# Moving weights stored as even and odd halves, and read from the two halves by turns

## The chip, the cores and the metric

The kernel runs on one core of one Trainium2 chip (trn2). The metric is the device time in microseconds of one execution; smaller is better. Three runs of the kernel before took 576.83, 577.91 and 578.27 us, a median of 577.91 us.

## The reference

A two-layer decoder trunk over 256 tokens with 1024 features, all in float32. Layer 0 is block-sparse attention with 16 heads (with 256 tokens there is one block, so it is plain causal attention). Layer 1 is sliding-window attention with window 128, four shared key/value heads and learned sinks. Each layer ends with a gated feed-forward block whose hidden rows pass a causal convolution of width 3:

```
for l in range(DEPTH):
    h = rmsnorm(x, attn_norm[l])
    if l < N_A:                       # layer 0
        q, k, v = split(h @ w_qkv_a[l], 3);  o = moba_attention(rope(q), rope(k), v)
    else:                             # layer 1
        k, v = split(rmsnorm(x, kv_norm) @ w_kv_b, 2)
        o = swa_sink_attention(rope(h @ w_q_b), rope(k), v, sinks_b)
    x = x + o @ w_o
    u = causal_conv3(rmsnorm(x, ffn_norm[l]) @ w_up[l])      # 1024 -> 2 x 2816
    gate, val = split(u, 2)
    x = x + (silu(gate) * val) @ w_down[l]                   # 2816 -> 1024
return rmsnorm(x, final_norm)
```

## The kernel before

**Products in three.** [...] To keep float32 accuracy, each operand is split into a high part (ScalarE copies it to float32r, L157) and a low part (VectorE subtracts, L160), and each product is three matmuls: high by high, high by low, low by high. In the profile `wh`/`wl` are the parts of a weight unit, and the tiles called `q` hold the parts of activations.

**Weight units.** The host packs all weights into 92 units of 128 partitions x 2048 columns (`pack`), 1 MB each. SyncE's queue fetches a unit into one of three `raw` buffers; ScalarE and VectorE make `wh` and `wl` in pieces; four pairs of them are in use or ready. When TensorE has used a unit, `used(i)` lets the preparation of unit i+4 begin. Tiles from `spaced` start 4 elements (16 bytes) into a buffer that is 64 elements longer than its content.

**Two kinds of matmul.** In the first kind the weights are stationary and the activations are the moving operand, 256 columns (the tokens): the q and k projections of layer 0 (`proj_f`, L445 to L447) and the up projections (L715 to L717). In the second kind the activations are stationary, 128 tokens at a time, and the weights are the moving operand. The second kind is what the change touches:

| place | lines | what | moving columns | matmuls |
|---|---|---|---|---|
| `v_first` | L827 | first half of layer 0's v, while weights still come in | 512 | 48 |
| `proj` | L317 to L319 | second half of v; layer 1's k and v | 512 | 96 |
| `proj` | L317 to L319 | layer 1's q, four groups | 256 | 192 |
| `Down.mm` | L621, L622, L626 | both attention outputs and both down projections | 512 | 714 |
| `Down.end` | L681 to L683 | last quarter of the last down projection | 256 | 12 |

Each matmul reads its columns one after the other from consecutive addresses of SBUF and adds to a PSUM bank in the same order.

**Order.** The order on each engine is fixed when the program is built. A small planner counts TensorE time (`tick`) and puts the conversions and the post-processing at due times between the matmuls. During attention, the softmax of one head pair runs beside matmuls that a `filler` generator gives: the other q/k groups, v, and the first units of the output projection.

Of the kernel before, what the change touches and what calls it, by code (L numbers as in the profile page):

```python
# [14 lines left out]
P = 128  # L15
D = 1024
S = 256
NB = S // P
KC = D // P
NH = 16  # L20
HD = 64
# [39 lines left out]
def trunk(ctx: ExitStack, tc, x, xw, pos, cpk, fin, sinks, w, out):  # L61
    nc = tc.nc
# [28 lines left out]
    def bank(tag):  # L91
        return ps.tile([P, 512], F32, tag=tag, name=nm(tag), bufs=4 if tag == "acc" else 2)
# [4 lines left out]
    def blk(b):  # L97
        return slice(b * P, (b + 1) * P)

    def half(n):  # L100
        return slice(n * 512, (n + 1) * 512)

# [11 lines left out]
    def tick(ns):  # L116
        clock[0] += ns
        while put_off and not busy[0]:
            item = min(put_off, key=lambda t: t[0])
            if item[0] > clock[0]:  # L120
                return
            run_item(item)
# [13 lines left out]
    def require(*key):  # L136

        while True:
            mine = [t for t in put_off if t[1] == key]
            if not mine:  # L140
                return
            run_item(min(mine, key=lambda t: t[0]))
# [45 lines left out]
    def used(i):  # L188

        prepare(i + 4)  # L190

    def need(i):
        require("w", i)
# [5 lines left out]
    first = [wp.tile([P, UNIT], F32, tag="raw", name=f"first{i}", bufs=3) for i in range(3)]  # L199
# [42 lines left out]
    for b in range(NB):  # L242
        t = one.tile([P, NH, HD], F32, name=f"v{b}")
# [62 lines left out]
    def hx(hT, c):  # L306
        hi, lo = hT[c // 4]
        return hi[:, c % 4], lo[:, c % 4]

    def proj(o, hT, b, wv, units=()):  # L310

        n = o.shape[-1]
        for c in range(KC):
            require("x", b, c // 4)
            xh, xl = hx(hT, c)
            wh, wl = wv(c)
            nc.tensor.matmul(o, xh[:, blk(b)], wh, start=(c == 0), stop=False)  # L317
            nc.tensor.matmul(o, xh[:, blk(b)], wl, start=False, stop=False)
            nc.tensor.matmul(o, xl[:, blk(b)], wh, start=False, stop=(c == KC - 1))  # L319
            tick(3 * n / 2.4)  # L320
            if units and (c + 1) * len(units) % KC == 0:
                used(units[(c + 1) * len(units) // KC - 1])
            yield 3 * n / 2.4
# [278 lines left out]
    class Down:  # L602
# [6 lines left out]
        def mm(self, i, k, b, cols):  # L609
            if self.acc is None:  # L610
                self.acc = [[bank("acc") for _ in range(2)] for _ in range(NB)]
            need(self.u + i)
            self.wait(i)
            hi, lo = wq[self.u + i]
            ph, pl = self.parts[2 * i + k]
            first = i == 0 and k == 0
            end = k == 1 and (i == self.n_u - 1 or i == self.n_u - 2 and self.short and (b, cols[0][0]) == (1, 1))
            for n, c in cols:
                o = self.acc[b][n][:, c]
                s_ = slice(k * D + n * 512 + c.start, k * D + n * 512 + c.stop)  # L620
                nc.tensor.matmul(o, ph[:, blk(b)], hi[:, s_], start=first, stop=False)  # L621
                nc.tensor.matmul(o, ph[:, blk(b)], lo[:, s_], start=False, stop=False)  # L622
            for n, c in cols:
                o = self.acc[b][n][:, c]
                s_ = slice(k * D + n * 512 + c.start, k * D + n * 512 + c.stop)
                nc.tensor.matmul(o, pl[:, blk(b)], hi[:, s_], start=False, stop=end)  # L626
            tick(len(cols) * 3 * (c.stop - c.start) / 2.4)

        def units(self, lo, hi):
# [37 lines left out]
        def end(self, b, n, tail):  # L667

            i = self.n_u - 1
            require("x", b, n)  # L670
            x_ = xr[b][:, half(n)]
            nc.vector.tensor_tensor(out=x_, in0=self.acc[b][n], in1=x_, op=ALU.add)
            need(self.u + i)
            self.wait(i)
            wh, wl = wq[self.u + i]
            for m in range(2):
                o = bank("u")[:, :S]
                for k in range(2):
                    ph, pl = (t[:, blk(b)] for t in self.parts[2 * i + k])
                    c = slice(k * D + n * 512 + m * S, k * D + n * 512 + (m + 1) * S)  # L680
                    nc.tensor.matmul(o, ph, wh[:, c], start=(k == 0), stop=False)  # L681
                    nc.tensor.matmul(o, ph, wl[:, c], start=False, stop=False)
                    nc.tensor.matmul(o, pl, wh[:, c], start=False, stop=(k == 1))  # L683
                tick(640)
                tail(m, o)

# [9 lines left out]
    def ffn(layer, u_up, u_dn, hT, y, rb, after, tail=None):  # L696
# [72 lines left out]
        for cs_ in (range(4), range(4, KC)):  # L769
            for i in range(2):  # L770
                mm(i, ups[i], cs_)
# [5 lines left out]
        for i in range(2, NF):  # L777
            if i % 2 == 0:
                pq = quad()
            up = bank("acc" if i < 4 else "t" if i % 2 else "u")  # L780
            mm(i, [up[:, :S], up[:, S:]], range(KC))
            used(u_up + i)
            post(i, [up[:, :S], up[:, S:]], pq)
# [35 lines left out]
    v_acc = [bank("acc") for _ in range(NB)]  # L819

    def v_first(c):
        xh, xl = hx(hT, c)
        s_ = slice((c % 4) * 512, (c % 4 + 1) * 512)
        wh, wl = (t[:, s_] for t in wq[c // 4])
        for k, (a, m) in enumerate(((xh, wh), (xl, wh), (xh, wl))):
            for b in range(NB):
                nc.tensor.matmul(v_acc[b], a[:, blk(b)], m, start=(c == 0 and k == 0), stop=(c == KC - 1 and k == 2))  # L827
        tick(1280)

    def v_out(b, n, o):  # L830
# [124 lines left out]
    def v_half(n, u):  # L955
        for b in range(NB):
            o = bank("acc")
            yield from proj(o, hT, b, cols512(u), (u, u + 1) if b else ())
            chain(("v", n), (150.0, lambda b=b, o=o: v_out(b, n, o)))
# [71 lines left out]
    for b in range(NB):  # L1031
        o = bank("acc")
# [94 lines left out]
def pack(inp):  # L1127

    import numpy as np

    def k_major(m):
        return m.reshape(m.shape[0] // P, P, m.shape[1])

    units = []
    m = k_major(inp["w_qkv_a"][0])
    q, k, v = (m[:, :, i * D:(i + 1) * D] for i in range(3))
    qk = [np.concatenate([q[:, :, g * 256:(g + 1) * 256], k[:, :, g * 256:(g + 1) * 256]], axis=2) for g in range(4)]
    blocks = [v[:, :, :512], qk[0], qk[1], qk[2], v[:, :, 512:], qk[3]]

    def halves(blk):  # L1140
        for a in range(2):
            units.append(blk[4 * a:4 * a + 4].transpose(1, 0, 2).reshape(P, UNIT))

    def rows2(mat):
        mm = k_major(mat)
        for i in range(mm.shape[0] // 2):
            units.append(mm[2 * i:2 * i + 2].transpose(1, 0, 2).reshape(P, UNIT))

    def up(mat):
        mm = k_major(mat).reshape(KC, P, 2, NF, P)  # L1150
        for i in range(NF):
            units.append(mm[:, :, :, i].transpose(1, 0, 2, 3).reshape(P, UNIT))

    for blk in blocks:
        halves(blk)
    rows2(inp["w_o_a"][0])
    up(inp["w_up"][0])
    rows2(inp["w_down"][0])
    halves(k_major(inp["w_kv_b"]))

    order = [(2 * (j // 4) + e) * 4 + j % 4 for j in range(NH // 2) for e in range(2)]
    m = k_major(inp["w_q_b"][0].reshape(D, NH, HD)[:, order].reshape(D, D))
    for g in range(4):
        units.append(m[:, :, g * 256:(g + 1) * 256].transpose(1, 0, 2).reshape(P, UNIT))
    rows2(inp["w_o_b"][0].reshape(NH, HD, D)[order].reshape(D, D))
    up(inp["w_up"][1])
    rows2(inp["w_down"][1])
    assert len(units) == N_UNITS
    wpk = np.stack(units)

    def feat(v_):
        return v_.reshape(-1, P).T

    cols = [feat(v_) for v_ in (inp["kv_norm"], inp["attn_norm"][1],
                                inp["ffn_norm"][0], inp["ffn_norm"][1])]
    for l in range(2):
        four = np.concatenate([inp["conv_w"][l], inp["conv_b"][l][None]], axis=0)
        cols.append(four.reshape(4, 2 * NF, P).transpose(2, 1, 0).reshape(P, 2 * NF * 4))
    cpk = np.concatenate(cols, axis=1)
    return {  # L1180
        "x": inp["x"].reshape(S, D),
        "xw": np.concatenate([feat(inp["attn_norm"][0])] + [
            t for c in range(KC) for t in (inp["x"].reshape(S, KC, P)[:, c].T, blocks[0][c])], axis=1),
        "pos": inp["positions"].reshape(NB, P).T,
        "cpk": cpk,
        "fin": inp["final_norm"],
        "sinks": inp["sinks_b"].reshape(NH)[order],
        "w": wpk,
    }
# [19 lines left out]
```

## Time and profile before

| what | value |
|---|---|
| time, median of 3 runs | 577.91 us (576.83 to 578.27) |
| span of the profiled execution, first to last instruction | 576.2 us; the median run stands 1.7 us above it (the profiled execution's own device time is not listed) |
| PE (matmul) busy | 560.7 us, 4022 instructions |
| VectorE / ScalarE / GpSimd busy | 438.0 / 379.5 / 103.5 us |
| HBM read | 99.30 MB, 174 GB/s over the span |
| mean granted TensorE clock | 0.989 |

PE counts as busy while any matmul is in flight, and neighbouring matmuls overlap: a row that says that one matmul took 390 ns does not mean that the next starts 390 ns later. How fast TensorE really goes is read from the distance between the starts of neighbouring matmuls, in the timeline and in the chain of waits. The chain of waits leads back from the last instruction of the program to what held each step.

### The profile page before, as it was taken

Reading aid. Unit: us, or ns where it says so; the run is one execution under the profiler, and the core shown is the slowest. Engines: PE = TensorE matmul, PEld = TensorE weight load, DVE = VectorE, ACT = ScalarE, POOL = GpSimd, SP = SyncE. Lnnn points to the kernel's source line nnn. Section 1 sums busy time; section 2 is a strip of 40 time slices with the busy share of each in tenths; the row PEclk is TensorE's granted clock in tenths of the full one; section 3 lists DMA queues with packets and bytes.
Section 4 is the critical chain, followed back from the end, with each engine's and each line's share of the span. In section 5 each row is a group of like instructions: output and inputs, shape, how many; then the busy total and the mean of one; then the engine's idle time right before and its main releaser. Section 6 shows DMA issues by size and latency. Waiting matters only on the chain.

```text
span 576.2 us, 10530 instructions
## 1 busy us (share of the span) xinstructions
PE 560.7 (97%) x4022; PEld 514.7 (89%) x4022; DVE 438.0 (76%) x928; ACT 379.5 (66%) x771; POOL 103.5 (18%) x130
## 2 busy tenths in 40 slices
PE   9789999999999999999999999999999999999995
PEld 7679889789999999988887988779999999988884
DVE  6579988678899888864449989778988888873414
ACT  6845987777567776752439788887666777663313
POOL 8221102002233223110000100001322322110003
PEclk9889999999999999999999999999999999999998
DMA  8834462532384656664551732323365556665201
GB/s 326 345 110 183 148 239 82 197 140 93 128 289 159 220 211 220 220 208 175 202 207 46 270 136 94 127 97 124 110 222 212 204 214 216 251 215 204 95 0 73
DMA packets 15312, 101.00 MB, mean 175 GB/s; under 512 B 1952, under 2 KB 2080, under 8 KB 3744
## 3 DMA queue, kind: packets, MB, share of 16 engines
q1 hardware_dynamic: 14976, 100.09, 48.5%
q8 instruction: 31, 0.51, 0.3%
q10 hardware_dynamic: 288, 0.26, 0.1%
q14 instruction: 17, 0.14, 0.1%
HBM read 99.30 MB, written 1.05 MB: 174 GB/s over the span
## 4 chain that ended last, share of the span: by engine, by line
PE 89%; ACT 3%; DVE 3%; DMA 2%; issue 1%; POOL 1%; SPq 0%; DVEq 0%; POOLq 0%; ACTq 0%
PE acc L621 9%; PE acc L622 9%; PE acc L626 9%; PE u L715 6%; PE u L717 6%; PE u L716 6%; PE t L717 6%; PE t L715 6%; PE t L716 6%; PE acc L447 2%; PE acc L445 2%; PE acc L446 2%; PE acc L715 2%; PE acc L717 2%; PE acc L716 2%; PE acc L317 2%
## 5 line engine op out<-in xcount | busy, mean ns | idle before, releaser
L160 DVE TENSOR_TENSOR wl<-wr,wh 128x1024 fp32r<-128x1024 f32 (+1 forms) x208 | 223.1, 1090 | 69.9 <-ACT wh L157 68.7
L157 ACT ACTIVATE wh<-wr 128x1024 fp32r<-128x1024 f32 (+1 forms) x208 | 189.6, 945 | 68.7 <-PE acc L626 56.5
L759 POOL TENSOR_TENSOR m<-m,m 128x256 f32<-128x256 f32 x44 | 63.8, 1449 | 177.2 <-DVE m L754 111.6
L621 PE MATMUL acc<-wh,q 128*128 128x512 f32 x238 | 94.3, 396 | 0.0
L622 PE MATMUL acc<-wl,q 128*128 128x512 f32 x238 | 92.8, 390 | 0.0
L715 PE MATMUL u<-q,wh 128*128 128x256 f32 x320 | 88.4, 277 | 0.0
L716 PE MATMUL u<-q,wh 128*128 128x256 f32 x320 | 88.2, 276 | 0.0
L717 PE MATMUL u<-q,wl 128*128 128x256 f32 x320 | 88.0, 275 | 0.0
L717 PE MATMUL t<-q,wl 128*128 128x256 f32 x288 | 79.2, 275 | 0.0
L715 PE MATMUL t<-q,wh 128*128 128x256 f32 x288 | 79.2, 275 | 0.0
L716 PE MATMUL t<-q,wh 128*128 128x256 f32 x288 | 79.2, 275 | 0.0
L626 PE MATMUL acc<-wh,q 128*128 128x512 f32 x238 | 77.1, 389 | 0.0
L716 PEld LDWEIGHTS u<-q,wh 128*128 128x128 f32 x320 | 60.1, 188 | 0.0
L717 PEld LDWEIGHTS u<-q,wl 128*128 128x128 f32 x320 | 60.1, 188 | 0.0
L715 PEld LDWEIGHTS u<-q,wh 128*128 128x128 f32 x320 | 59.9, 188 | 0.0
L717 PEld LDWEIGHTS t<-q,wl 128*128 128x128 f32 x288 | 54.1, 188 | 0.0
L715 PEld LDWEIGHTS t<-q,wh 128*128 128x128 f32 x288 | 54.1, 188 | 0.0
L716 PEld LDWEIGHTS t<-q,wh 128*128 128x128 f32 x288 | 54.1, 188 | 0.0
L621 PEld LDWEIGHTS acc<-wh,q 128*128 128x128 f32 x238 | 44.7, 188 | 9.6 <-issue 0.9
L626 PEld LDWEIGHTS acc<-wh,q 128*128 128x128 f32 x238 | 44.7, 188 | 9.3
L622 PEld LDWEIGHTS acc<-wl,q 128*128 128x128 f32 x238 | 44.7, 188 | 8.5 <-issue 0.2
L763 ACT ACTIVATE q<-m 128x256 fp32r<-128x256 f32 x44 | 18.1, 415 | 38.7 <-POOL m L759 38.7
(187 smaller groups left out, 1136.0 us busy)
## 6 DMA issues: line engine op xcount, KB each, us to landing
wr<-in_w SPq DMA_DIRECT2D x90, 1024.0 KB, 4.8
first<-in_xw SPq DMA_DIRECT2D x5, 384.0 KB, 5.6
xr<-in_x SPq DMA_DIRECT2D x2, 512.0 KB, 8.4
first<-in_xw SPq DMA_DIRECT2D x1, 768.0 KB, 7.0
fin_t<-in_fin SPq DMA_DIRECT2D x1, 512.0 KB, 5.6
out<-ot SPq DMA_DIRECT2D x1, 512.0 KB, 2.6
first<-in_xw SPq DMA_DIRECT2D x1, 388.0 KB, 3.4
out<-m ACTq DMA_DIRECT2D x1, 256.0 KB, 2.1
```

Source lines behind the costliest of these rows:

```text
L157: nc.scalar.activation(wq[i][0][:, c], raws[i][:, c], AF.Copy)
L160: nc.vector.tensor_tensor(out=wq[i][1][:, c], in0=raws[i][:, c], in1=f(wq[i][0][:, c]), op=ALU.subtract)
L317: nc.tensor.matmul(o, xh[:, blk(b)], wh, start=(c == 0), stop=False)
L445: nc.tensor.matmul(om, wh, xh, start=(c == 0), stop=False)
L621: nc.tensor.matmul(o, ph[:, blk(b)], hi[:, s_], start=first, stop=False)
L622: nc.tensor.matmul(o, ph[:, blk(b)], lo[:, s_], start=False, stop=False)
L626: nc.tensor.matmul(o, pl[:, blk(b)], hi[:, s_], start=False, stop=end)
L715: nc.tensor.matmul(o, hi[:, s_], xh, start=(c == 0), stop=False)
L716: nc.tensor.matmul(o, hi[:, s_], xl, start=False, stop=False)
L717: nc.tensor.matmul(o, lo[:, s_], xh, start=False, stop=(c == KC - 1))
L759: nc.gpsimd.tensor_tensor(out=h, in0=gs, in1=t[1], op=ALU.mult)
L763: (3400.0, lambda: nc.scalar.activation(hi, h, AF.Copy)),
```

## The change

The host stores the moving weights in another column order: in each group of 512 columns (256 for layer 1's q) the even columns come first and the odd ones behind them. The kernel reads a group as two halves by turns: first column of the first half, first column of the second half, second column of the first half, and so on. TensorE thus sees the same columns in the same order as before, and writes the same PSUM columns in the same order (`pairs` splits the output into pairs only so that its shape is that of the operand). What is different is the address of each column that is read: neighbours in time are now 1024 bytes apart in SBUF (512 bytes in layer 1's q, whose groups have 256 columns) where they were 4 bytes apart. Stationary weights, activations, conversions and DMAs are as before, and the instruction order on all five engines, with its waits, is the same.

```diff
+    def turns(ap):
+        return ap.rearrange("p (a t) -> p t a", a=2)
+
+    def pairs(ap):
+        return ap.rearrange("p (t a) -> p t a", a=2)
...
-            nc.tensor.matmul(o, xh[:, blk(b)], wh, start=(c == 0), stop=False)
-            nc.tensor.matmul(o, xh[:, blk(b)], wl, start=False, stop=False)
-            nc.tensor.matmul(o, xl[:, blk(b)], wh, start=False, stop=(c == KC - 1))
+            nc.tensor.matmul(pairs(o), xh[:, blk(b)], turns(wh), start=(c == 0), stop=False)
+            nc.tensor.matmul(pairs(o), xh[:, blk(b)], turns(wl), start=False, stop=False)
+            nc.tensor.matmul(pairs(o), xl[:, blk(b)], turns(wh), start=False, stop=(c == KC - 1))
...
-                nc.tensor.matmul(o, ph[:, blk(b)], hi[:, s_], start=first, stop=False)
-                nc.tensor.matmul(o, ph[:, blk(b)], lo[:, s_], start=False, stop=False)
+                nc.tensor.matmul(pairs(o), ph[:, blk(b)], turns(hi[:, s_]), start=first, stop=False)
+                nc.tensor.matmul(pairs(o), ph[:, blk(b)], turns(lo[:, s_]), start=False, stop=False)
...
-                nc.tensor.matmul(o, pl[:, blk(b)], hi[:, s_], start=False, stop=end)
+                nc.tensor.matmul(pairs(o), pl[:, blk(b)], turns(hi[:, s_]), start=False, stop=end)
...
-                    c = slice(k * D + n * 512 + m * S, k * D + n * 512 + (m + 1) * S)
-                    nc.tensor.matmul(o, ph, wh[:, c], start=(k == 0), stop=False)
...
+                    c = slice(k * D + n * 512, k * D + (n + 1) * 512)
+                    rh, rl = (turns(t[:, c])[:, m * P:(m + 1) * P] for t in (wh, wl))
+                    nc.tensor.matmul(pairs(o), ph, rh, start=(k == 0), stop=False)
...
-                nc.tensor.matmul(v_acc[b], a[:, blk(b)], m, start=(c == 0 and k == 0), stop=(c == KC - 1 and k == 2))
+                nc.tensor.matmul(pairs(v_acc[b]), a[:, blk(b)], turns(m), start=(c == 0 and k == 0),
+                                 stop=(c == KC - 1 and k == 2))
...
+    def turned(m, n=512):
+        s = m.shape
+        return m.reshape(*s[:-1], s[-1] // n, n // 2, 2).swapaxes(-1, -2).reshape(s)
...
+    v = turned(v)
...
-        mm = k_major(mat)
+        mm = turned(k_major(mat))
...
-    halves(k_major(inp["w_kv_b"]))
+    halves(turned(k_major(inp["w_kv_b"])))
...
-    m = k_major(inp["w_q_b"][0].reshape(D, NH, HD)[:, order].reshape(D, D))
+    m = turned(k_major(inp["w_q_b"][0].reshape(D, NH, HD)[:, order].reshape(D, D)), 256)
```

More of the change, by code (lines that the diff above doesn't have):

```diff
@@ L679, in end @@
                     ph, pl = (t[:, blk(b)] for t in self.parts[2 * i + k])
-                    c = slice(k * D + n * 512 + m * S, k * D + n * 512 + (m + 1) * S)
-                    nc.tensor.matmul(o, ph, wh[:, c], start=(k == 0), stop=False)
-                    nc.tensor.matmul(o, ph, wl[:, c], start=False, stop=False)
-                    nc.tensor.matmul(o, pl, wh[:, c], start=False, stop=(k == 1))
+                    c = slice(k * D + n * 512, k * D + (n + 1) * 512)
+                    rh, rl = (turns(t[:, c])[:, m * P:(m + 1) * P] for t in (wh, wl))
+                    nc.tensor.matmul(pairs(o), ph, rh, start=(k == 0), stop=False)
+                    nc.tensor.matmul(pairs(o), ph, rl, start=False, stop=False)
+                    nc.tensor.matmul(pairs(o), pl, rh, start=False, stop=(k == 1))
                 tick(640)
```

## The prediction

> **What bounds the kernel now.** I read the page first: the share of each engine, and the chain that ended last.
>
> ```profile
> PE 560.7 (97%) x4022; PEld 514.7 (89%) x4022; DVE 438.0 (76%) x928; ACT 379.5 (66%) x771; POOL 103.5 (18%) x130
> PE 89%; ACT 3%; DVE 3%; DMA 2%; issue 1%; POOL 1%; SPq 0%; DVEq 0%; POOLq 0%; ACTq 0%
> ```
>
> The first row has busy time, share of the span and instructions; the second has the share of each engine in the chain. TensorE is in flight for 97% of the span and is 89% of the chain, so almost any change of the matmuls' pace arrives in the time. Where it does not arrive is shown by the chain of waits in order of time (start, length, what):
>
> ```profile
> 16.80 2.20 ACT wh L157 x4
> ...
> 39.00 0.70 DVE wl L160
> 39.74 0.39 PE acc L447
> ...
> 510.78 0.45 PE acc L626 x2
> 512.14 0.45 PE acc L626 x2
> ...
> 558.38 0.45 PE acc L626 x2
> 567.27 0.65 issue
> 567.92 1.31 POOL xf L1079
> ```
>
> Up to 39.74 us it goes through conversions on ScalarE and VectorE; from there to about 567 us it is TensorE, and a tail of 9 us follows. The windows view (length, then busy time and instructions of each engine, granted clock, DMA share, GB/s) shows the same for two stages of moving weights, the second down projection and the second attention:
>
> ```profile
> 336.00:382.00 46.00, 44.57 (x328) 37.35 (x327) 37.55 (x136) 38.49 (x118) 0.00 (x0) 1.00 0.28 96
> ...
> 508.00:566.00 58.00, 58.00 (x266) 48.34 (x265) 24.48 (x30) 19.77 (x26) 3.64 (x4) 1.00 0.31 109
> ```
>
> In the down projection TensorE has no gap, while VectorE and ScalarE work less than half the time and the DMA engines 0.31 of it: nothing else can set the pace there. Attention has gaps of 1.4 us in 46, and VectorE and ScalarE are over 80% busy.
>
> Now the pace itself. In the chain, the two L626 rows at 510.78 and 512.14 are six matmuls of 512 columns apart, and from 510.78 to 558.38 us lie 35 such steps: 47.60 us / 210 = **226.7 ns a matmul**, 0.443 ns a column. The up projection, whose moving operand is activations, has the same pace per column (timeline: start, length):
>
> ```profile
> 479.78 0.28 PE L715 MATMUL u<-q,wh 128*128 128x256 f32 x1
> ...
> 485.90 0.28 PE L715 MATMUL t<-q,wh 128*128 128x256 f32 x1
> ```
>
> That is 54 matmuls of 256 columns in 6.12 us: 113.3 ns each, again 0.443 ns a column. The cost goes with the columns and not with the matmul. A third place has the clock halved, just after a gap at 26 us:
>
> ```profile
> 26.00:28.80 2.80, 2.80 (x15) 2.80 (x14) 1.99 (x3) 2.80 (x7) 0.00 (x0) 0.50 0.22 83
> ...
> 26.47 0.41 PE L446 MATMUL acc<-q,wh 128*128 128x256 f32 x1
> ...
> 28.82 0.41 PE L445 MATMUL acc<-q,wh 128*128 128x256 f32 x1
> ```
>
> Here the clock is 0.50, and 11 steps take 2.35 us: 213.6 ns per 256 columns, 0.834 ns a column. At clock 1.00 this scales to 0.417 ns a column: 106.8 ns per 256 and 213.6 per 512. The measured pace is 6% slower than that, one lost cycle in about 17. So **at full clock the array is not the limit; the columns do not arrive fast enough**. The second up projection has this load beside it:
>
> ```profile
> 400.00:505.00 105.00, 105.00 (x929) 105.00 (x928) 91.61 (x150) 74.72 (x122) 30.21 (x20) 1.00 0.55 197
> ```
>
> VectorE is 87% busy there, ScalarE 71%, DMA 0.55, each about twice what it is in the down projection (42%, 34%, 0.31), and the pace per column is the same. So the loss is no collision with them. It is a property of how one run of consecutive columns is read.
>
> [...]
>
> **The change part by part.** No instruction is added, removed or moved on any engine, and the planner's numbers are as before; conversions and DMAs handle the same bytes. The packing is on the host, outside the metric. What changes is the pace at which the moving weights arrive. The groups affected (page and groups by shape; count, busy us and mean ns):
>
> ```profile
> L621 PE MATMUL acc<-wh,q 128*128 128x512 f32 x238 | 94.3, 396 | 0.0
> L622 PE MATMUL acc<-wl,q 128*128 128x512 f32 x238 | 92.8, 390 | 0.0
> ...
> L626 PE MATMUL acc<-wh,q 128*128 128x512 f32 x238 | 77.1, 389 | 0.0
> ...
> L317 PE MATMUL acc<-wh,q 128*128 128x256 f32 x64 | 18.7, 292 | 0.0
> ...
> L317 PE MATMUL acc<-wh,q 128*128 128x512 f32 x32 | 12.8, 401 | 0.0
> ...
> L827 PE MATMUL acc<-wh,q 128*128 128x512 f32 x32 | 9.5, 423 | 0.0
> ...
> L681 PE MATMUL u<-wh,q 128*128 128x256 f32 x4 | 1.1, 276 | 0.0
> ```
>
> With 512 columns: 3 x 238 = 714 (`Down.mm`), 3 x 32 = 96 (`proj`; L318 and L319 are as many) and 48 (`v_first`, 32 and 16 with `wl`), together 858. With 256: 3 x 64 = 192 (`proj`) and 3 x 4 in `Down.end`, together 204. The 48 of `v_first` lie before 39.74 us, where the chain goes over conversions: they are worth nothing. That leaves 810 and 204.
>
> The price of a turned column is in no row, as no matmul here reads its moving operand in steps. I bound it from both sides:
>
> - From below, it can't be faster than the array: 0.417 ns a column, from the half-clock rows. 810 x (226.7 - 213.6) + 204 x (113.3 - 106.8) = 10.6 + 1.3 = **11.9 us gained**.
> - From above, by the slowest pace of columns in these rows, 0.834 ns: 810 x 200.3 + 204 x 100.3 = 162 + 20 = **183 us lost**, and up to 10 more from `v_first`, whose 48 x 200 ns would then outlast the conversions.
>
> Which end? The row that I take as nearest is the transposes in attention, from the chain:
>
> ```profile
> 364.68 0.66 PE u L548 x6
> ```
>
> Six matmuls of 128 columns in 0.66 us are 110 ns each, 0.859 ns a column: a run of addresses taken at half the pace. Against twice the array's 53.4 ns, 106.8, they lose 3 ns each, and per matmul, not one cycle in 17. The half-clock rows lose nothing either. So a run of neighbouring addresses that is drained at 1.2 columns per ns keeps up, and at 2.4 it falls to 2.26. Read by turns, each half gives 1.2 columns per ns. If the limit belongs to the place that is read, the change puts each place below it. I therefore take the lower end and leave 3 ns a matmul as the transposes show: 216.6 ns for 512 columns and 109.8 for 256. 810 x 10.1 + 204 x 3.5 = 8.2 + 0.7 = **8.9 us**.
>
> What hides part of it: about 192 of the 512s (second v half, three units of each output projection) and 144 of the 256s stand in attention as filler beside the softmax; that is 1.9 + 0.5 = 2.4 us. TensorE's waits there were 1.4 us in 46, so softmax is nearly late already; when the filler gets shorter, the transposes L548 wait for the exponentials. I leave a quarter of this out: 0.6 us. In the down projections a unit's 24 matmuls shrink from 5.44 to 5.20 us; a unit's fetch takes 4.8 us to land (first row below), three buffers take them by turns, and the conversions (second row, the first down projection: 11.35 and 9.30 us in 24) have room, so nothing new is late.
>
> ```profile
> wr<-in_w SPq DMA_DIRECT2D x90, 1024.0 KB, 4.8
> ...
> 258.00:282.00 24.00, 24.00 (x108) 19.87 (x107) 11.35 (x10) 9.30 (x10) 0.00 (x0) 1.00 0.55 205
> ```
>
> Sum: 8.9 - 0.6 = 8.3 us off the profiled span of 576.2, to 567.9. The median of the runs, 577.91, stands 1.7 above the span; the same 8.3 off it gives **569.6 us**.
>
> **The rivals.**
>
> *Each turned column needs a read of its own (slower).* If SBUF gives TensorE a group of neighbouring columns at one access, consecutive columns are served from it, and by turns every access goes elsewhere. At one access per column the pace can drop to the 0.834 ns of the half-clock rows or the 0.859 of the transposes: 183 to 192 us more, a time of 761 to 770, and 90 or so more if only half of that is lost (about 670). It decides as soon as a turned column costs more than 0.443 ns, since 810 x 512 + 204 x 256 = 467,000 columns on the path make 4.7 us for each 0.01 ns. For it speaks that the only fast stages in the trace read consecutive addresses; against it, that the loss of one in 17 comes in exactly this pattern, so consecutive addresses have a price of their own.
>
> [...]
>
> *The limit is TensorE's read port, not the place (no change).* If the port passes 2.26 float32 columns per ns whatever their addresses, every turned matmul keeps 226.7 ns and the time stays at 577.9. For it: the same 0.443 ns for weights and activations, at all addresses and beside any traffic. Against it: nothing but that the read order is untested. It is also what would be seen if the pattern were merged somewhere so that nothing changed at the memory.
>
> **How the numbers follow.** About 0.3% (1.7 us) is what a measurement of this kernel can tell from no change. My forecast (the loss goes, in whole or for the most part) has 0.47, the port 0.17, an access per column 0.36. The forecast by itself spans 565 (all 11.9 us and a low run) to 574 (half of it). Of the third case about 0.10 lies between 580 and 750, 0.18 at 750 to 772, the rest higher. A range that holds 8 in 10 must reach into it: **564 to 772**. Predicted: **569.6 us**; faster 0.47, same 0.17, slower 0.36.
>
> **What would show it.** Right: in the chain, neighbouring L626 pairs stand 1.28 to 1.30 us apart instead of 1.36, the up projection keeps 113.3 ns, and the second down projection ends about 2.6 us sooner relative to its start. Port: 1.36 stays. An access per column: 1.36 becomes 2.5 or more, the granted clock still 1.00, and VectorE's and ScalarE's shares fall in these stages. My forecast would be wrong above all if the loss of one cycle in 17 is made on TensorE's side of the read, or if neighbouring columns come in one access.

## The result, and the profile after

The changed kernel takes 570.18 us (median; 569.15 to 571.11) against 577.83 (576.83 to 578.27): a ratio of **0.9871, 95% interval 0.9853 to 0.9888**, 7.5 us faster (6.5 to 8.5). Timed a second time it gave 0.9878 (0.9859 to 0.9896). The profiled execution has a span of 567.4 us against 576.2, 8.8 less; it was the fastest of its kernel's runs.

The page of the changed kernel, the rows of busy time and of the chain by engine:

```profile
PE 550.1 (97%) x4022; PEld 512.6 (90%) x4022; DVE 437.0 (77%) x928; ACT 379.0 (67%) x771; POOL 104.0 (18%) x130
PE 84%; DVE 7%; ACT 4%; DMA 2%; issue 1%; POOL 1%; SPq 0%; DVEq 0%; POOLq 0%; ACTq 0%
```

The same 4022 matmuls are in flight 10.6 us less; the other engines have the same work. TensorE's share of the chain fell from 89% to 84% and VectorE's rose from 3% to 7%: somewhere VectorE now comes last. The chain of waits in the second down projection (start, length, what; L633 is L626 of before):

```profile
542.23 0.43 PE acc L633 x2
543.52 0.43 PE acc L633 x2
...
550.00 0.43 PE acc L633 x2
```

Six matmuls now take 1.295 us instead of 1.36: **215.8 ns each instead of 226.7**. Where the 8.8 us came from is read from the timeline, at the first matmul of each stage. Before, with layer 0's q and k, its up projection, its down projection, layer 1's k and v, the second up and down projections and the very last quarter:

```profile
16.66 0.28 PE L445 MATMUL acc<-q,wh 128*128 128x256 f32 x1
...
125.16 0.48 PE L715 MATMUL u<-q,wh 128*128 128x256 f32 x2
...
246.15 0.40 PE L621 MATMUL acc<-wh,q 128*128 128x512 f32 x1
...
307.51 0.48 PE L317 MATMUL acc<-wh,q 128*128 128x512 f32 x1
...
388.72 0.48 PE L715 MATMUL u<-q,wh 128*128 128x256 f32 x2
...
509.70 0.40 PE L621 MATMUL acc<-wh,q 128*128 128x512 f32 x1
...
568.20 0.28 PE L681 MATMUL u<-wh,q 128*128 128x256 f32 x1
```

The same seven places of the changed kernel:

```profile
16.31 0.29 PE L452 MATMUL acc<-q,wh 128*128 128x256 f32 x1
...
122.69 0.48 PE L723 MATMUL u<-q,wh 128*128 128x256 f32 x2
...
243.67 0.38 PE L628 MATMUL acc<-wh,q 128*128 128x512 f32 x1
...
302.30 0.46 PE L324 MATMUL acc<-wh,q 128*128 128x512 f32 x1
...
382.67 0.49 PE L723 MATMUL u<-q,wh 128*128 128x256 f32 x2
...
503.64 0.38 PE L628 MATMUL acc<-wh,q 128*128 128x512 f32 x1
...
559.33 0.27 PE L689 MATMUL u<-wh,q 128*128 128x256 f32 x1
```

Differences of neighbouring starts give the stages:

| stage | before us | after us | difference | turned matmuls x saving each |
|---|---|---|---|---|
| to layer 0's q, k | 16.66 | 16.31 | -0.35 | 48, expected to be worth nothing |
| q, k, first attention, its output | 108.50 | 106.38 | -2.12 | 144 x 10.9 ns = 1.57 |
| up projection 0 | 120.99 | 120.98 | -0.01 | none |
| down projection 0 | 61.36 | 58.63 | -2.73 | 264 x 10.9 ns = 2.88 |
| k, v, q, second attention, its output | 81.21 | 80.37 | -0.84 | 144 x 10.9 + 192 x 1.6 ns = 1.88 |
| up projection 1 | 120.98 | 120.97 | -0.01 | none |
| down projection 1, to its last quarter | 58.50 | 55.69 | -2.81 | 258 x 10.9 ns = 2.81 |
| last quarter and tail | 8.00 | 8.07 | +0.07 | 12 |

The down projections give 5.5 of the 8.8 us, matmul by matmul. The stages with no turned matmul give nothing.

The first two rows hold more than the change. The chain first reaches TensorE for good at 39.74 us before and at 38.83 after, behind conversions of the same work. In a second trace of the changed kernel (e8 below; span 569.2 us) this is at 40.37 us and the first up projection begins at 124.49, while all its later stages agree with the "after" column within 0.03 us. From where TensorE takes over to the up projection it is 85.42 us before and 83.86 and 84.12 after, so 1.3 to 1.6 us for the 1.57 of the table. From there to the end of the program the change gives 7.9 us by the first trace and 7.6 by the second, which agrees with the ratio; the other 0.9 of the 8.8 us are an early start of that execution.

Only the second attention falls clearly short. Its windows, before and then after (length, busy time of PE, PEld, DVE, ACT, POOL, clock, DMA share, GB/s):

```profile
307.50:388.70 81.20, 79.65 (x559) 68.05 (x558) 70.52 (x242) 69.14 (x198) 3.81 (x6) 1.00 0.38 133
```

```profile
302.30:382.60 80.30, 77.80 (x557) 67.28 (x557) 70.31 (x243) 68.93 (x198) 3.83 (x6) 1.00 0.40 134
```

TensorE's busy time fell by 1.85 us and the stage by 0.9: its gaps grew from 1.55 to 2.50 us, while VectorE and ScalarE had 70.3 and 68.9 us of work in either. The chain shows the difference. Before, it leaves TensorE in this stage only between about 331 and 352 us:

```profile
309.82 0.44 PE t L264 x2
...
322.33 0.41 PE t L358 x2
...
332.01 0.40 DVE m L507
```

After, it leaves TensorE at 296.5 us, ahead of the stage, passes mostly through VectorE's parts of activations and weights to about 317 us, and through both engines again from 325 to 354:

```profile
296.54 0.64 ACT m L283 x2
...
312.52 1.49 DVE wl L167 x2
314.26 1.48 DVE wl L167 x2
...
333.41 0.40 ACT m L540
```

Off TensorE it spends some 21 of 81 us before and 43 of 80 after.

### The profile page after: what moved, and what is told of

It is laid out like the page before. It is cut to its first block, busy times and chain, and to the rows that moved or that the text cites. A ratio compares the mean times of both kernels' runs of the same rounds, so it can differ in the third digit from the quotient of the medians.

```text
span 567.4 us, 10530 instructions
## 1 busy us (share of the span) xinstructions
PE 550.1 (97%) x4022; PEld 512.6 (90%) x4022; DVE 437.0 (77%) x928; ACT 379.0 (67%) x771; POOL 104.0 (18%) x130
## 4 chain that ended last, share of the span: by engine, by line
PE 84%; DVE 7%; ACT 4%; DMA 2%; issue 1%; POOL 1%; SPq 0%; DVEq 0%; POOLq 0%; ACTq 0%
PE acc L628 9%; PE acc L629 9%; PE acc L633 9%; PE u L725 6%; PE u L724 6%; PE u L723 6%; PE t L725 6%; PE t L724 6%; PE t L723 6%; DVE wl L167 3%; PE acc L452 2%; PE acc L454 2%; PE acc L453 2%; PE acc L724 2%; PE acc L723 2%; PE acc L725 2%
## 5 line engine op out<-in xcount | busy, mean ns | idle before, releaser
L628 PE MATMUL acc<-wh,q 128*128 128x512 f32 x238 | 92.0, 386 | 0.0
L629 PE MATMUL acc<-wl,q 128*128 128x512 f32 x238 | 90.6, 380 | 0.0
L723 PE MATMUL u<-q,wh 128*128 128x256 f32 x320 | 88.4, 277 | 0.0
L723 PE MATMUL t<-q,wh 128*128 128x256 f32 x288 | 79.2, 275 | 0.0
L633 PE MATMUL acc<-wh,q 128*128 128x512 f32 x238 | 74.6, 379 | 0.0
L723 PEld LDWEIGHTS u<-q,wh 128*128 128x128 f32 x320 | 59.9, 188 | 0.0
L723 PEld LDWEIGHTS t<-q,wh 128*128 128x128 f32 x288 | 54.1, 188 | 0.0
L628 PEld LDWEIGHTS acc<-wh,q 128*128 128x128 f32 x238 | 45.0, 189 | 7.0 <-issue 0.9
L633 PEld LDWEIGHTS acc<-wh,q 128*128 128x128 f32 x238 | 45.0, 189 | 6.3
L629 PEld LDWEIGHTS acc<-wl,q 128*128 128x128 f32 x238 | 45.0, 189 | 5.9 <-issue 0.2
```

The lines of the kernel that those rows point to most:

```text
L628: nc.tensor.matmul(pairs(o), ph[:, blk(b)], turns(hi[:, s_]), start=first, stop=False)
L629: nc.tensor.matmul(pairs(o), ph[:, blk(b)], turns(lo[:, s_]), start=False, stop=False)
L633: nc.tensor.matmul(pairs(o), pl[:, blk(b)], turns(hi[:, s_]), start=False, stop=end)
L723: nc.tensor.matmul(o, hi[:, s_], xh, start=(c == 0), stop=False)
```

## The experiments

Wherever columns are exchanged, shifted, repeated or left out below, the output differs from the reference; instructions and their order stay. The pace of a form is read from the timeline: a unit of a down projection has 24 matmuls and a block of an up projection 48, so the distance of the first rows of two neighbours, divided by that, is start to start of one.

### Which orders lose the cycle (e1)

```diff
+    LAYER0 = [                                  # unit i of layer 0's down projection
+        lambda o, l, r, **k: mmul(o, l, r, **k),                    # L616, d = 1
+        lambda o, l, r, **k: mmul(seq(o, 2), l, by(r, 2), **k),     # L617, d = 2
...
+    LAYER1 = [                                  # layer 1's
+        lambda o, l, r, **k: mmul(cont(o, 2), l, step(r, 2), **k),  # L627, s = 2
...
-                nc.tensor.matmul(o, ph[:, blk(b)], hi[:, s_], start=first, stop=False)
+                mul(o, ph[:, blk(b)], hi[:, s_], start=first, stop=False)
```

`by(r, d)` reads column 0, d, 1, d+1, and so on within blocks of 2d columns; `step(r, s)` reads 0, s, 2s, and then from 1.

> The kernel before, with the moving weights of the first nine units of each down projection read in another order (packing and PSUM order as before, so the columns of these products are exchanged, and in the last two forms repeated, and the output is another). Layer 0, units 0 to 8: two neighbouring runs of d columns by turns, d = 1 (plain), 2, 4, 8, 16, 32, 64, 128, 256. Layer 1: every s-th column, s = 2, 4, 8, 16, 32, 64, 128; then one column 512 times; then 256 columns, each twice in succession. Start to start of one 512-column matmul. Plain must give 226.7 ns and d = 256 216, as in the two kernels. Theory A (a place of a certain size gives at most 2.26 columns per ns, two places by turns give more): 216 only from some distance on, about 227 below it, and step 2 and 4 stay near 227. Theory B (only an unbroken run of consecutive addresses loses the cycle): 216 for every d from 2 on and for every step. Theory C (a group of 4 neighbouring columns comes in one access, and turning to another group costs an access): d = 4 and more and all steps from 4 on cost 216 at best and some over 227. One column repeated, and each column twice: 216 if reading is what loses the cycle; 227 if the loss is in the array or in writing PSUM.

First row of each unit, start and modelled length of one matmul; L616 to L624 are d = 1 to 256, L637 is plain:

```profile
246.55 0.40 PE L616 MATMUL acc<-wh,q 128*128 128x512 f32 x1
252.01 0.39 PE L617 MATMUL acc<-wh,q 128*128 128x512 f32 x1
257.45 0.38 PE L618 MATMUL acc<-wh,q 128*128 128x512 f32 x1
262.62 0.38 PE L619 MATMUL acc<-wh,q 128*128 128x512 f32 x1
...
288.52 0.38 PE L624 MATMUL acc<-wh,q 128*128 128x512 f32 x1
293.70 0.39 PE L637 MATMUL acc<-wh,q 128*128 128x512 f32 x1
```

Layer 1: L627 is step 2, L628 step 4, L633 step 128, L634 one column 512 times, L635 each of 256 twice:

```profile
508.24 0.61 PE L627 MATMUL acc<-wh,q 128*128 128x512 f32 x1
519.10 0.64 PE L628 MATMUL acc<-wh,q 128*128 128x512 f32 x1
...
573.23 0.45 PE L633 MATMUL acc<-wh,q 128*128 128x512 f32 x1
...
579.85 0.38 PE L634 MATMUL acc<-wh,q 128*128 128x512 f32 x1
...
585.03 0.38 PE L635 MATMUL acc<-wh,q 128*128 128x512 f32 x1
```

5.46 and 5.44 us for d = 1 and 2 are 227 ns a matmul; from d = 4 on it is 5.17 to 5.19 us, 215.8. The halves are not needed: **a distance of 4 columns, 16 bytes, does all of it**. One column repeated takes 215.8 too (579.85 to 585.03), so the lost cycle is in reading and not in the array or PSUM. Nor is it the pairing of the output columns: d = 2 has that too, and gains nothing. Steps are the surprise: 452 ns for step 2 (10.86 us a unit), 460 for 4, 431 to 494 for 8 to 64, and 276 for 128, which reads four places by turns. Theory B falls (d = 2, all steps). A falls by the steps, and C by the turns, which change the group of 4 at each read and are the fastest of all.

### Activations, and the floor at 256 columns (e2)

```diff
+    UP = {
+        6: lambda o, l, r, **k: mmul(pairs(o), l, turns(r), **k),
+        8: lambda o, l, r, **k: mmul(o, l, r[:, :1].to_broadcast([P, S]), **k),
...
-                    nc.tensor.matmul(o, hi[:, s_], xh, start=(c == 0), stop=False)
+                    mul(o, hi[:, s_], xh, start=(c == 0), stop=False)
```

> The kernel before, with another read order of the 256 moving activation columns in four blocks of both up projections (the tokens of these blocks are exchanged or repeated, so the output is another): block 6 the two halves by turns; block 8 one column 256 times; block 10 128 columns, each twice in succession; block 16 every 4th column. Start to start of one 256-column matmul is 113.3 ns when plain. Theory A and B: by turns 111.7, as layer 1's q in the changed kernel. If the rest above 106.7 is still reading, one column repeated gives 107 to 109; if something else, such as loading the stationary operand, sets a floor, it gives 111.7 too. If activations in a q tile behaved in another way than weights, by turns would stay at 113.3.

Block 6 (L705) and the plain block behind it (L710), up to block 8 (L706):

```profile
159.56 0.38 PE L705 MATMUL u<-q,wh 128*128 128x256 f32 x2
...
164.91 0.40 PE L710 MATMUL t<-q,wh 128*128 128x256 f32 x2
...
170.36 0.38 PE L706 MATMUL u<-q,wh 128*128 128x256 f32 x2
```

By turns 5.35 us for 48, 111.5 ns; plain 5.45 us, 113.5. One column repeated and each column twice gave 111.6 as well, every 4th column 232.9. Activations behave as weights do, and what is left above the 106.8 ns of the half-clock rows is not the reading of the moving columns, since one column repeated has it too.

### More orders (e3)

```diff
+        (0, lambda o, l, r, **k: mmul(runs(o, 2), l, blocks(r, 2), **k)),   # L616: 0 1 256 257 2 3 ...
...
+        (2, lambda o, l, r, **k: mmul(seq(o, 4), l, by(r, 4), **k)),        # L621: d = 4, moved by 2
...
+                s_ = slice(k * D + n * 512 + c.start + e, k * D + n * 512 + c.stop + e)
```

> The kernel before, with more read orders of the 512 moving weights in the first nine units of each down projection (columns of these products are exchanged or shifted, so the output is another). The first look gave 226.7 ns for consecutive columns and for turns over a distance of 2, 215.8 for turns over 4 to 256, and 430 to 490 for steps from 2 to 64. Theory L: columns at even and at odd places of the order are fetched separately, each with its own last-read group of 4 columns (16 bytes, aligned); consecutive order uses each group twice per fetch and just fails to keep up, turns over 4 or more use it four times, steps once. Theory W: two groups are kept whatever the place in the order, and a turn between two groups hides the fetch of the next. Layer 0: blocks of b columns from the two halves by turns, b = 2, 4, 8, 16, 64. L: b = 2 changes the group at each read of both lanes, 274 or more (what four places gave), b = 4 and more use each group twice, 226.7. W: b = 2 and 4 are as fast as single turns, 215.8. Then turns over d = 4, 8, 16 with all columns moved by 2 columns (8 bytes), and d = 4 moved by 1. L: moved by 2, d = 4 uses a group twice: 226.7; d = 8 and 16 lie between, at 216 to 222. W: 215.8 for all. Layer 1: four places by turns over d = 4, 8, 16, 32, 64. Both: slower than 226.7, about the 274 of d = 128. Consecutive moved by 1 and by 2: both 226.7. Four places, d = 4, moved by 2: slower than without. Turns over 64 moved by 2: 216.

L616 to L620 are blocks of 2, 4, 8, 16, 64; L621 to L623 are d = 4, 8, 16 moved by 2 columns, L624 d = 4 moved by 1:

```profile
245.02 0.51 PE L616 MATMUL acc<-wh,q 128*128 128x512 f32 x1
252.90 0.43 PE L617 MATMUL acc<-wh,q 128*128 128x512 f32 x1
...
276.00 0.39 PE L621 MATMUL acc<-wh,q 128*128 128x512 f32 x1
281.47 0.39 PE L622 MATMUL acc<-wh,q 128*128 128x512 f32 x1
...
292.21 0.43 PE L624 MATMUL acc<-wh,q 128*128 128x512 f32 x1
298.63 0.41 PE L637 MATMUL acc<-wh,q 128*128 128x512 f32 x1
```

Blocks of 2 take 328 ns (7.88 us a unit): theory W, which said 215.8, falls. d = 4 moved by 2 columns takes 228 (5.47 us), as L said: turning over 16 bytes helps only when the groups of 4 are met at their borders. Four places take 268 to 274, as before. L missed in size: blocks of 4, 8 and 16 took 250, 244 and 240 (it said 226.7), d = 8 moved by 2 took 226 (said up to 222), d = 4 moved by 1 took 267, turns over 64 moved by 2 took 221 (said 216), and consecutive columns moved by 1 or 2 took 234 (said 226.7). Four places over d = 4, moved by 2, took 338, slower than the 268 without, as expected.

### Counting reads per group (e6)

```diff
+        (0, lambda o, l, r, **k: mmul(flat(o, 2), l, halves_by(r, 2), **k)),    # L613: 0 256 2 258 ...
+        (0, lambda o, l, r, **k: mmul(flat(o, 4), l, halves_by(r, 4), **k)),    # L614: 0 256 4 260 ...
...
+        (0, lambda o, l, r, **k: mmul(turned(o, r, 384)[0], l, turned(o, r, 384)[1], **k)),   # L629
```

> The kernel before, with further read orders of the 512 moving weights in the down projections (columns exchanged, shifted, repeated or left out, so the output is another). Theory L, in its count form: each of two lanes (even and odd places of the order) reads 256 columns, and what counts is how often in succession a lane reads from the same aligned group of 4 columns: four times 215.8 ns, twice 226.7, once 430 or more. Theory P: what counts is that neighbours in the order lie in two places at least 16 bytes apart. Layer 0: the two halves by turns, but each half read with step 2: L 226.7, P 215.8; with step 4 and step 8: L 430 or more, P 215.8; 256 columns with step 2, each twice: L 226.7; four places in another order: 268 to 274 as before; consecutive from 4 columns on (16 bytes): 226.7; from 3 columns on: 234 as with 1 and 2 (the start inside a group costs 7 ns, not explained by either); halves by turns moved by 2 columns: 220 as the turns over 64 moved by 2; moved by 4: 215.8. Layer 1, for the floor at 256 columns: by turns with 384, 320 and 256 columns, then consecutive with 384, 320, 256. If a matmul costs N/2.4 + 2.5 ns and never less than a weight load of 111.7: 162.5, 135.8, 111.7 by turns, and 170, 141.7, 113.3 consecutive. If the fixed part grows in short matmuls (5 ns at 256): 384 by turns would be 164 or more, and 320 137 or more.

L613, L614, L615 are the halves by turns, each with step 2, 4, 8:

```profile
246.78 0.40 PE L613 MATMUL acc<-wh,q 128*128 128x512 f32 x1
252.23 0.61 PE L614 MATMUL acc<-wh,q 128*128 128x512 f32 x1
263.09 0.64 PE L615 MATMUL acc<-wh,q 128*128 128x512 f32 x1
```

Step 2 takes 227 ns (5.45 us), step 4 452 (10.86 us): two distant places by turns are **not** enough, and theory P falls. The count of L holds: 256 columns with step 2, each twice, took 228 (said 226.7). The halves moved by 2 columns took 216 (said 220), moved by 4, 215.8. Consecutive columns moved by 3 and by 4 took 232, with single starts 220 to 240 ns apart, as the timeline gives them to 10 ns; the whole 16 bytes should have left 226.7. Now fewer columns, by turns 384, 320, 256 (L629 to L631), then L632:

```profile
527.69 0.32 PE L629 MATMUL acc<-wh,q 128*128 128x384 f32 x1
531.59 0.30 PE L630 MATMUL acc<-wh,q 128*128 128x320 f32 x1
534.85 0.27 PE L631 MATMUL acc<-wh,q 128*128 128x256 f32 x1
537.53 0.34 PE L632 MATMUL acc<-wh,q 128*128 128x384 f32 x1
```

162.5, 135.8 and 111.7 ns. The first two and the 215.8 of 512 turned columns lie on one line: 0.417 ns a column, as the half-clock rows scale to, and 2.5 ns a matmul, the N/2.4 + 2.5 of the expectation. The third lies above it, where the line gives 109.2: a floor. Consecutive, 384, 320 and 256 columns took 170.4, 146.3 and 118.8 (said 170, 141.7 and 113.3); why the last two are slower is open.

### The floor and the weight load (e7)

```diff
+        6: lambda o, t, s, r, **k: mmul(o, t[:, s][:, :1].to_broadcast([P, P]), r, **k),    # L718
+        8: lambda o, t, s, r, **k: mmul(o, every(t, s, 2), r, **k),                         # L719
+        10: lambda o, t, s, r, **k: mmul(o, every(t, s, 4), r, **k),                        # L720
```

> The kernel in which the up projections' activations are read by turns too, with the stationary weights of four blocks of both up projections taken in another way (the output is another): block 6 one column 128 times, block 8 every second column, block 10 every 4th, block 12 every 16th. Start to start of a 256-column matmul is 111.7 ns otherwise. If the floor of 111.7 is the weight load's reading, with lanes as for the moving operand: one column repeated gives 109.2 (N/2.4 + 2.5), steps give 220 or more. If the load goes by columns at a fixed pace whatever their addresses: 111.7 in all four. If the load is no part of the floor: 111.7 for the repeated column, and the steps change nothing until a load takes longer than 111.7.

Blocks 6 and 10 and the usual ones behind them (L723):

```profile
158.25 0.39 PE L718 MATMUL u<-q,wh 128*128 128x256 f32 x2
...
163.61 0.39 PE L723 MATMUL t<-q,wh 128*128 128x256 f32 x2
...
180.02 0.63 PE L720 MATMUL u<-q,wh 128*128 128x256 f32 x2
...
191.32 0.39 PE L723 MATMUL t<-q,wh 128*128 128x256 f32 x2
```

The stationary operand with step 4 doubles the time to 235 ns (11.30 us for 48); step 16 gave 221 and step 2 118.5. One column repeated stays at 111.7. So the load, one per matmul, does set the pace when it is slow: its rows (PEld) have 331 ns with step 4, 314 with step 16 and 192 as usual. That 111.7 ns is what a load of 128 stationary columns takes at best is the reading that fits, as the order of the moving columns (e2) and a repeated stationary column change nothing; a matmul with a shorter load, which would show it, was not run. None of the three expectations had this whole: steps do count, though a repeated column gains nothing.

### Only the down projections and outputs (e5)

```diff
-            nc.tensor.matmul(pairs(o), xh[:, blk(b)], turns(wh), start=(c == 0), stop=False)
+            nc.tensor.matmul(o, xh[:, blk(b)], wh, start=(c == 0), stop=False)
...
-    v = turned(v)
```

> The changed kernel with v, layer 1's k, v and q as before the change: only the four products of Down read by turns. Of the span's 8.8 us, 714 matmuls at 10.9 ns account for 7.8. If softmax in the second attention swallows what the shorter q and k, v give, the span is 568 to 568.7 and the time about 571; if their full worth arrives (96 x 10.9 + 192 x 1.7 and what the q groups ran above 113.3 ns, some 2 us), the span is 569.5 and the time 572.

0.9881 (0.9862 to 0.9899), 570.44 us, span 567.8: the same as the whole change within the intervals. Layer 1's stage took 80.51 us in its trace, against 80.37 with k, v and q turned and 81.21 before. What the turned k, v and q of layer 1 save is swallowed, nearly all of it. The first 16 us are the same without `v_first` turned (layer 0's q and k begin at 16.2 us).

### Turning the activations too (e4, e8, e9)

```diff
+                hi, lo = (split(part[:, c])[:, :, :, b * HD:(b + 1) * HD] for part in hT[n])
+                src = y_.rearrange("p c (t a) -> p c a t", a=2)
...
-                    nc.tensor.matmul(o, hi[:, s_], xh, start=(c == 0), stop=False)
+                    nc.tensor.matmul(pairs(o), hi[:, s_], turns(xh), start=(c == 0), stop=False)
```

> The changed kernel, with the 256 moving activation columns of both up projections also stored as two halves (ScalarE and VectorE write them so, reading every second token) and read by turns; the rest as in the changed kernel. The 1824 matmuls of the up projections go from 113.3 to 111.7 ns, the pace that turned and repeated columns had: 3.0 us less than the changed kernel, 567.2 us, ratio to before 0.982. Rival: reading every second token slows ScalarE's and VectorE's parts; there are 8 pieces a layer and block, most off the path, so at most 1 us of it is given back (568). If the second rival of the prediction held for activations (the port), the time would be the changed kernel's 570.2.

0.9833 (0.981 to 0.9856), 568.50 us. Then beside the changed kernel:

> The changed kernel itself once more, beside the next one on the same chip: 0.987 of the kernel before, about 569.7 us.

> The kernel with the up projections' activations by turns too, beside the changed kernel. Its up projections were 119.8 us each in the trace against 121.0 in the changed kernel: 2.2 us less in all, a ratio to before of 0.983 to 0.984. If the difference seen before came from the runs' spread, the two are equal.

**0.9824 (0.9807 to 0.9841) against 0.9878 (0.9859 to 0.9896)**, 567.39 and 570.71 us: the intervals don't meet, so this version beats both kernels, the changed one by about 3 us. In e4's trace the up projections took 119.7 and 119.8 us from their first matmul to their last, instead of 120.9 in the changed kernel: 2.2 us together. The expectation counted 1824 matmuls and 3.0 us, but both up projections together have 2112, which at 1.6 ns make 3.4: about a third of it does not arrive, and why was not looked into. The port rival is out for activations too.

## Why the prediction was right

- **What bounds the kernel.** Right in the main. The stages of pure TensorE gave what the number of matmuls times the saving says (2.81 and 2.81 us in the second down projection, 2.73 and 2.88 in the first), and the tail did not move. One reading was wrong: the chain before is not TensorE's from 39.74 to 567 us, but goes over ScalarE and VectorE from about 331 to 352, in the second attention.
- **"The columns do not arrive fast enough."** Right, and now shown: one column 512 times loses nothing (215.8 ns), the same matmul with 512 consecutive columns takes 226.7.
- **"If the limit belongs to the place that is read."** The outcome was right and this reason only half. Distance is not what helps: 16 bytes do as well as 1024 (e1), and two places 1024 bytes apart lose twofold when each is read with step 4 (e6). In most orders the pace went by how often in succession the even places of the order, and apart from them the odd ones, read from one aligned group of 4 columns (16 bytes): four times 215.8, twice 226.7 to 228, once 431 to 494, in steps of 2 to 64 and in halves with step 4 or 8. Consecutive columns use a group twice for each of the two. That there are two such readers is inferred from these times. It does not explain why places met again (four places, 268 to 274; blocks of 2, 328) cost less than steps, nor the 240 to 250 of blocks of 4 to 16, nor the 232 to 235 of consecutive columns that start elsewhere. That is open.
- **The nearest row.** The transposes (110 ns for 128 columns) were a lucky guide: the runs show no rule that a place read at half the pace keeps up. The row can also be read in another way: each transpose has a weight load of 128 columns too, and 110 ns is near the floor of 111.7 that e6 and e7 show for matmuls of twice as many moving columns. Which of the two it is stays open.
- **Size.** 512 columns: 216.6 said, 215.8 measured. 256: 109.8 said, 111.7 measured, a floor that the sum did not have and that is most likely the weight load's. Without anything hidden this makes 810 x 10.9 + 204 x 1.6 = 9.2 us instead of 8.9.
- **What attention hides.** 0.6 us were left out for both. The second lost 1.0 of its 1.88 (and the q groups, which ran at up to 120 ns before and at 112 after, should have added to these); the first gave 1.3 to 1.6 of its 1.57, by the two traces of the changed kernel. The place was right and the way only in part: TensorE's waits at the transposes for ScalarE (L548, L555 after), which the prediction named, grew from 1.3 to 1.5 us, and most of the other new gaps lie in the first 19 us of the stage, of which the chain now spends 15 on VectorE. That VectorE and ScalarE set the pace in the second attention is read from the chain and from e5; a run with less work on them was not made.
- **Sum.** 8.3 us said; 7.5 (6.5 to 8.5) by the ratio, 7.6 to 7.9 in the traces from where TensorE takes over. 569.6 us said, 570.18 measured. Two errors cancel in part: the saving was taken 0.3 us too low, and what attention hides 0.4 or more too low. The range up to 772 us was that wide because the prediction could not exclude the slower case; only the sum was a test of the mechanism.
- **The rivals.** The port is out: the order changes the pace. The price that the half-clock rows gave to one access per column (427 ns) is nearly met, but in other orders: step 4, which leaves each group after one read, takes 460. (At 0.859 ns a column that rival's sum is 194 us more, not 192.) Going elsewhere at every access is not by itself what costs: in this change each read goes to another group of 4 columns than the last, and it is the fastest (215.8), while step 2 reads each group twice running and takes 452.

## What to carry to other kernels

When matmuls follow each other without a gap and still come slower than the clock allows (here 226.7 ns for 512 columns, against the 213.6 that the half-clock rows scale to), compare with rows at half clock and look at how the moving operand is read: a loss that went with the columns, at any load of the other engines, was here one of reading order. For float32r moving operands, read two runs by turns, each aligned to 16 bytes and at least 16 bytes from the other (215.8 ns for 512 columns in e1, d = 4 to 256), with the output columns in order, as in every form run here; avoid steps of 2 to 64 columns (431 to 494 ns in e1). Weights packed on the host get this for nothing; in a stage where the chain of waits goes over VectorE or ScalarE, expect little of it (the second attention gave 0.84 of 1.88 us).

## What the runs showed that was not expected

- A step of 2 float32 columns in the moving operand doubles a matmul (452 ns for 512 columns instead of 226.7), while a step of 128, four places by turns, costs only a fifth (276).
- A stationary operand with step 4 doubles a matmul as well: 235 ns instead of 111.7 for 256 columns.
- Consecutive reading has a slower form besides 226.7 and 113.3: 118.8 ns for 256 columns in e6, up to 120 in layer 1's q before the change, 232 to 235 for 512 columns that start 1 to 4 columns further on. Turned columns that start at a group's border never showed it (111.7 and 215.8).
